# Time mixing in groups of two pairs of heads, issued by a timetable, with the keys projected ahead of it

## The chip, the cores and the metric

The kernel runs on one core of one Trainium2 chip. The metric is the device time of one execution in microseconds (us); the time of a kernel is the median of its runs. Five engines run side by side, each through its own list of instructions in that list's order: TensorE (PE in the profile: matrix products into PSUM; its weight loads are shown as PEld), VectorE (DVE), ScalarE (ACT), GpSimd (POOL) and SyncE (SP, which here only issues DMAs). They wait for each other by semaphores.

## The reference

The program is a trunk of two layers over one sequence of 256 tokens with a width of 2048. Layer 0 is RWKV-7 time mixing, layer 1 is chunked band attention over keys and values that are projected once; each is followed by a squared-ReLU MLP of width 8192. Every sub-layer has an RMS norm in front, shifted and scaled by vectors that come from a condition `c` through `c @ w_ada` (twelve such vectors of 2048 in the two layers, two more for the shared keys), and a gate from the same product on its output. All is f32. The change concerns time mixing:

```
xr, xw, xk, xv, xa, xg = [h + (shift(h) - h) * mu[j] for j in range(6)]
r, k, v = xr @ w_r, xk @ w_k, xv @ w_v
w_log = -softplus(-(w0 + tanh(xw @ w1) @ w2)) - 0.5
a = sigmoid(a0 + (xa @ a1) @ a2);  g = sigmoid(xg @ g1) @ g2
kk = normalized(k * k_k);  k = k * (1 + (a - 1) * k_a);  decay = exp(-exp(w_log))
for t in range(256):                      # 32 heads of 64, S is 64 x 64
    sa = S @ (-kk[t])
    S  = S * decay[t] + sa (kk[t] * a[t])' + v[t] k[t]'
    y[t] = S @ r[t]
y = groupnorm(y) * ln_w + ln_b + sum(r * k * r_k) * v
out = (y * g) @ w_o
```

## The kernel before

**Dense products.** A weight tile of 128x1024 f32 (half of the 2048 rows that one output tile of 128 needs, in eight blocks of 128x128) arrives by one DMA of 512 KB in a buffer `raw`. ScalarE rounds it to `wH`, VectorE makes the rest `wL = raw - wH` (`halves`, lines L360 and L363), and the activations are split in the same manner (`aHL`). For each block TensorE multiplies `wH` by both parts of the activation, 512 columns (L394), and `wL` by the upper part, 256 columns (L395). Such a pair of products is called a step here: an output tile of 128 takes 16 steps, a weight half 8. There are 6 buffers `raw` and 3 each of `wH` and `wL`.

**The condition's vectors.** `ada` takes one tile of 128x1024 of `w_ada` through a `raw` buffer, and VectorE adds it, scaled, to `acc` (L423). Sixteen tiles give half a vector; `ada_sum` then adds over the partitions with 32 small products. There are 384 tiles. Calls of `ada()` are strewn over the whole kernel, and `ada_need(...)` runs what is missing of a vector at once before its use.

**Time mixing.** Two heads fill the 128 partitions and are a pair; there are 16 pairs. The recurrence runs in 4 chunks of 64 tokens. `Pair` has three stages, written as generators: `early` (decays, normalized keys: long chains of elementwise work with `s` buffers), `invert` (the Gram products of keys, `gr`, and the inverse of a triangular matrix of 64 by doubling: five levels, each a product of 32x32 tiles, a copy `xs` on ScalarE, a second product, an addition to `u` and a transpose `tt` on VectorE), and `late` (the state `zs` from chunk to chunk, `chn`, the outputs `py`, the norm and the gate). In a period of 16 slots one pair is projected (`proj_steps`: `k` and `r`, 32 steps), the pair before it is in `early`, the one before that in `invert`, the one before that in `late`. There are 19 periods; in the last three, parts of the output projection (`out_steps`) take the place of the projections. `ADA_SLOTS` puts six tiles of `w_ada` in each period from the third.

**Order.** The code only says what depends on what. A scheduler that goes by the order of the code and by its own estimates sets the order of every engine's list; `issue_after` holds the small products and the dense steps of neighbouring slots together on TensorE.

The stage before time mixing projects `v` and ends at 221.7 us in the trace; after it come the output projection (`out_proj`), the first MLP, the attention and the second MLP.

Of the kernel before, what the change touches and what calls it, by code (L numbers as in the profile page):

```python
# [17 lines left out]
P = 128  # L18
D = 2048
T = 256  # L20
# [12 lines left out]
        "w0", "a0", "k_k", "k_a", "r_k", "ln_w", "ln_b"]  # L33
# [3 lines left out]
def _constants():  # L37
# [23 lines left out]
    p = np.arange(P)  # L61
    bones = (p[:, None] // C == p[None, :] // C).astype(np.float32)
    put("bones", bones)
# [10 lines left out]
class Pair:  # L74
# [3 lines left out]
    EARLY = 8  # L78

    def __init__(self, body, j, v, tw, ta, tg, e01):  # L80
        self.b, self.j, self.v, self.tw, self.ta, self.tg, self.e01 = body, j, v, tw, ta, tg, e01
        self.heads = (slice(0, C), slice(C, P))

    def s(self, name="s", bufs=10):
        return self.b.pw.tile([P, T], F32, tag=name, bufs=bufs, name=name)

    def big(self, name, bufs):
        return self.b.pw.tile([P, 4, P], F32, tag=name, bufs=bufs, name=name)

    @staticmethod  # L90
    def ch(t):
        return t.rearrange("p (c t) -> p c t", t=C)

    def each(self, o, lhsT, rhs):
        for c in range(4):
            for K in self.heads:
                self.b.nc.tensor.matmul(o(c)[K], lhsT(c)[K], rhs(c)[K], start=True, stop=True)  # L97

    def tiles(self, o, lhsT, rhs, pairs):

        for c in range(4):
            for R, K in pairs:
                self.b.nc.tensor.matmul(o[QS[K], c, :], lhsT[QS[R], c, :], rhs[QS[R], c, :], start=True, stop=True,  # L103
                                        tile_position=(H * R, H * K))

    def parts(self, func, src, scale=1.0):

        nc, pw = self.b.nc, self.b.pw
        H, L = (pw.tile([P, T], F32R, tag=n, bufs=2, name=n) for n in ("sH", "sL"))
        nc.scalar.activation(H, src, func, scale=scale)  # L110
        if func != AF.Copy:
            t = self.s("pt", 2)
            nc.scalar.activation(t, src, func, scale=scale)
            src = t
        nc.gpsimd.tensor_tensor(out=L, in0=src, in1=H, op=ALU.subtract)  # L115
        return H, L

    def head_sums(self, ps, parts):
        for i, t in enumerate(parts):
            self.b.nc.tensor.matmul(ps, self.b.bones, t, start=(i == 0), stop=(i == 1))  # L120

    def early(self):
        b, nc, j, k, r, v, s, ch = self.b, self.b.nc, self.j, self.k, self.r, self.v, self.s, self.ch
        pw, vec, cst, e01 = b.pw, b.vec, b.cst, self.e01
        lw = pw.tile([96, 2, P], F32, tag="lw", bufs=2, name="lw")
        nc.sync.dma_start(out=lw, in_=b.d["lora2"][j, :96, 0:2])
        self.lg = pw.tile([P, 2, P], F32, tag="lg", bufs=2, name="lg")
        nc.sync.dma_start(out=self.lg, in_=b.d["lora2"][j, :, 2:4])
        z = b.psm()
        nc.tensor.matmul(z[:, 0:T], lw[:, 0, :], self.tw, start=True, stop=True)  # L130
        nc.tensor.matmul(z[:, T:2 * T], lw[:, 1, :], self.ta, start=True, stop=True)

        sw, a = s(), s()
        for o, at, b0 in ((sw, 0, "w0"), (a, T, "a0")):
            nc.vector.tensor_scalar(out=o, in0=z[:, at:at + T], scalar1=vec(b0, j), scalar2=-80.0,
                                    op0=ALU.add, op1=ALU.max)
            nc.scalar.activation(o, o, AF.Exp, scale=-1.0)
        yield
        sq = self.parts(AF.Square, k, vec("k_k", j))
        for o in (sw, a):  # L140
            nc.scalar.activation(o, o, AF.Ln, bias=b.col(C_ONE))
        nc.scalar.activation(sw, sw, AF.Exp, scale=-1.0, bias=b.col(C_MHALF))
        nc.scalar.activation(a, a, AF.Exp, scale=-1.0)
        yield
        pss = b.psm()[:, :T]
        self.head_sums(pss, sq)
        cum = s()
        nc.vector.tensor_tensor_scan(out=cum, data0=cst("reset"), data1=sw, initial=0.0, op0=ALU.mult, op1=ALU.add)
        e0, e1 = e01[:, :, 0:C], e01[:, :, 1:C + 1]
        nc.scalar.activation(e1, ch(cum), AF.Exp, scale=-1.0)  # L150
        e2 = s()
        nc.scalar.activation(e2, cum, AF.Exp)
        self.pc = pw.tile([P, 4, 1], F32, tag="pc", bufs=3, name="pc")
        nc.gpsimd.tensor_copy(self.pc, e01[:, :, C:C + 1])
        yield
        rs, ss, rr = s(), s(), s()
        nc.vector.tensor_scalar(out=ss, in0=pss, scalar1=1e-24, scalar2=None, op0=ALU.max)
        nc.scalar.activation(rs, ss, AF.Ln)
        nc.scalar.activation(rs, rs, AF.Exp, scale=-0.5)
        nc.scalar.activation(rr, rs, AF.Square)  # L160
        km = s()
        nc.gpsimd.tensor_scalar(out=km, in0=a, scalar1=-1.0, scalar2=vec("k_a", j), op0=ALU.add, op1=ALU.mult)
        self.bh, self.kh = s("bh", 2), s("kh", 2)
# [927 lines left out]
```

## Time and profile before

| | us |
|---|---|
| median of 3 runs (2776.5 to 2784.27) | 2779.97 |
| the profiled execution | 2773.6 |
| its span | 2771.8 |
| projection of `v` and what lies before it | 0 to 221.7 |
| time mixing, up to the last pair's output | 221.7 to 761.6 |
| rest of the output projection | 761.6 to 839.7 |
| first MLP | 839.7 to 1593.2 |
| attention | 1593.2 to 2037.9 |
| second MLP and end | 2037.9 to 2771.8 |

The profiled execution stands 0.23% under the median. Stages were cut where the first instruction of the next begins (the first dense step, the last write of `v`, the first normed tile of the next norm). A trace shows each instruction with its start and duration, the idle time before it and what ended that. An f32 product is recorded twice, so that 16 products show as x32. Ends of products are modelled: two that follow each other overlap in the records, so the cost of one is the distance to the start of the next.

### The profile page before, as it was taken

What the parts mean: (1) busy time and instruction counts of PE and PEld (TensorE: products, weight loads), DVE (VectorE), ACT (ScalarE), POOL (GpSimd) and SP (SyncE); (2) the same over time, 40 slices, a digit from 0 to 9 for tenths busy, and PEclk for the clock granted to TensorE, in tenths of its full rate; (3) what the DMA queues carried; (4) which work ended last, traced back from release to release, by engine and by line L of the source; (5) the groups of instructions that cost most, each with busy time, mean ns of one, the idle gap of its engine ahead of it and who ended that gap; (6) DMA issues with size and microseconds to landing.
All of it is one profiled execution on the core that took longest, in us unless ns stands there. A gap on an engine that the chain in (4) does not pass through costs nothing.

```text
span 2771.8 us, 57644 instructions
## 1 busy us (share of the span) xinstructions
PE 2653.9 (96%) x23402; PEld 2217.6 (80%) x23402; DVE 2087.3 (75%) x3098; ACT 1260.9 (45%) x2214; POOL 301.8 (11%) x416
## 2 busy tenths in 40 slices
PE   6998999999998999999999899999989999999997
PEld 3677777777887888888888788877878888888886
DVE  4568778878889888888788896799786566665665
ACT  2345555556344434344344354465444344443444
POOL 0003443443220000000000200000100000000002
PEclk9999999999999999999999999999999999999999
DMA  9886556555687888888888868888876555555553
GB/s 297 269 281 193 169 171 196 176 176 162 216 302 243 298 308 305 300 314 296 299 306 302 304 218 282 268 293 268 279 242 216 187 186 186 187 183 189 185 188 122
DMA packets 217387, 662.60 MB, mean 239 GB/s; under 512 B 21408, under 2 KB 68896, under 8 KB 217120
## 3 DMA queue, kind: packets, MB, share of 16 engines
q1 hardware_dynamic: 215056, 656.36, 71.5%
q8 instruction: 184, 3.01, 0.4%
q10 hardware_dynamic: 2064, 2.54, 0.3%
q14 instruction: 83, 0.68, 0.1%
HBM read 656.72 MB, written 2.10 MB: 238 GB/s over the span
## 4 chain that ended last, share of the span: by engine, by line
PE 76%; DVE 9%; DMA 7%; issue 4%; POOL 1%; ACT 1%; DVEq 0%; SPq 0%; ACTq 0%; POOLq 0%
PE pj L394 40%; PE pj L395 20%; DMA raw<-w_ada 5%; DVE wL L363 3%; DVE acc L423 2%; PE iv L103 2%; PE gr L97 1%; DMA raw<-w_ada_kv 1%; PE m L625 1%; DVE un L504 1%; PE o L383 1%; PE ms L97 1%; POOL sL L115 1%; PE chn L276 1%; DVE aHL L506 1%
## 5 line engine op out<-in xcount | busy, mean ns | idle before, releaser
L394 PE MATMUL pj<-aHL,wH 128*128 128x512 f32 x3712 | 1353.5, 405 | 26.0 <-DVE aHL L506 22.4
L360 ACT CAST wH<-raw 128x1024 fp32r<-128x1024 f32 x772 | 807.0, 1047 | 949.4 <-PE pj L394 622.1
L363 DVE TENSOR_TENSOR wL<-raw,wH 128x1024 fp32r<-128x1024 f32 x772 | 946.1, 1228 | 290.7 <-ACT wH L360 288.8
L395 PE MATMUL pj<-aHL,wL 128*128 128x256 f32 x3712 | 1049.3, 283 | 7.5 <-DVE wL L363 7.2
L394 PEld LDWEIGHTS pj<-aHL,wH 128*128 128x128 f32 x3712 | 700.3, 189 | 199.2 <-issue 28.0
L394 PE MATMUL pj<-hHL,wH 128*128 128x512 f32 x2048 | 722.0, 397 | 4.5 <-DVE hHL L882 4.5
L395 PEld LDWEIGHTS pj<-aHL,wL 128*128 128x128 f32 x3712 | 705.3, 190 | 14.6 <-DVE wL L363 11.9
L395 PE MATMUL pj<-hHL,wL 128*128 128x256 f32 x2048 | 574.3, 281 | 4.6 <-DVE wL L363 4.5
L423 DVE SCALAR_TENSOR_TENSOR acc<-raw,ct,acc 128x1024 f32<-128x1024 f32 x360 | 470.4, 1307 | 139.8 <-DMA raw<-w_ada 104.0
L394 PEld LDWEIGHTS pj<-hHL,wH 128*128 128x128 f32 x2048 | 384.3, 188 | 97.9 <-DVE hHL L882 6.7
L395 PEld LDWEIGHTS pj<-hHL,wL 128*128 128x128 f32 x2048 | 386.8, 189 | 8.1 <-DVE wL L363 7.7
L482 POOL TENSOR_TENSOR ss<-ss,sq 128x256 f32<-128x256 f32 x56 | 65.0, 1160 | 1599.7 <-ACT sq L481 1599.4
L901 DVE SCALAR_TENSOR_TENSOR x<-pj,mod,x 128x256 f32<-128x256 f32 x256 | 123.1, 481 | 51.7 <-PE pj L395 48.8
L881 ACT CAST hHL<-t 128x256 fp32r<-128x256 f32 x128 | 51.4, 403 | 67.6 <-DVE t L880 67.3
L625 PE MATMUL m<-rawa,crep 128*32 128x256 f32 x512 | 47.4, 449 | 17.5 <-DMA rawa<-w_ada 16.9
L481 ACT ACTIVATE sq<-x 128x256 f32<-128x256 f32 x60 | 25.0, 418 | 70.5 <-DVE x L901 39.6
L880 DVE SCALAR_TENSOR_TENSOR t<-t 128x256 f32<-128x256 f32 x128 | 53.9, 422 | 3.0
L882 DVE TENSOR_TENSOR hHL<-t,hHL 128x256 fp32r<-128x256 f32 x128 | 53.4, 418 | 0.6 <-ACT hHL L881 0.5
L862 DVE TENSOR_TENSOR t<-pj,t 128x256 f32<-128x256 f32 x128 | 53.2, 417 | 0.0
L239 POOL TENSOR_TENSOR al<-da,csts 128x128 f32<-128x128 f32 x64 | 40.7, 647 | 67.4 <-PE iv L103 62.7
L861 ACT COPY t<-pj 128x256 f32<-128x256 f32 x128 | 46.6, 366 | 0.0
L685 PE MATMUL t<-aHL,wH 128*128 128x256 f32 x128 | 38.1, 298 | 5.8 <-DVE v L693 3.6
(230 smaller groups left out, 2483.0 us busy)
## 6 DMA issues: line engine op xcount, KB each, us to landing
raw<-w_ada SPq DMA_DIRECT2D x320, 512.0 KB, 4.7
raw<-w_up SPq DMA_DIRECT2D x256, 512.0 KB, 4.9
raw<-w_down SPq DMA_DIRECT2D x256, 512.0 KB, 4.3
rawa<-w_ada SPq DMA_DIRECT2D x64, 512.0 KB, 6.8
raw<-w_ada_kv SPq DMA_DIRECT2D x64, 512.0 KB, 5.4
raw<-w_k SPq DMA_DIRECT2D x32, 512.0 KB, 4.2
raw<-w_r SPq DMA_DIRECT2D x32, 512.0 KB, 4.7
raw<-w_o SPq DMA_DIRECT2D x32, 512.0 KB, 5.2
```

The costliest lines, as they stand in the source:

```text
L97: self.b.nc.tensor.matmul(o(c)[K], lhsT(c)[K], rhs(c)[K], start=True, stop=True)
L103: self.b.nc.tensor.matmul(o[QS[K], c, :], lhsT[QS[R], c, :], rhs[QS[R], c, :], start=True, stop=True, tile_position=(H * R, H * K))
L360: nc.scalar.copy(Hf, raw)
L363: eng.tensor_tensor(out=Lf, in0=raw, in1=Hf, op=ALU.subtract)
L394: nc.tensor.matmul(ps, H[:, i, :], a(kt), start=(kt == 0), stop=False)
L395: ins = nc.tensor.matmul(ps[:, 0, :], L[:, i, :], a(kt)[:, 0, :], start=False, stop=(kt == KT - 1))
L423: nc.vector.scalar_tensor_tensor(out=acc, in0=raw, scalar=ck, in1=acc, op0=ALU.mult, op1=ALU.add)
L482: (eng or nc.gpsimd).tensor_tensor(out=self.ss, in0=self.ss, in1=sq, op=ALU.add)
L625: nc.tensor.matmul(ps[g:g + 32, part, :W], crep[:, kt, :], raw[:, i, :], start=(part == 1 and kt < 4), stop=(part == 0 and kt >= KT - 4), ...
L880: nc.vector.scalar_tensor_tensor(out=t, in0=t, scalar=0.0, in1=t, op0=ALU.max, op1=ALU.mult)
L882: nc.vector.tensor_tensor(out=h[:, 1, :], in0=t, in1=h[:, 0, :], op=ALU.subtract)
L901: nc.vector.scalar_tensor_tensor(out=x, in0=ps[:, i, :], scalar=self.mods[(layer, 5)][:, n:n + 1], in1=x, op0=ALU.mult, op1=ALU.add)
```

## The change

Time mixing is written anew. A `Quad` holds two pairs, so that elementwise work goes over 512 columns where it went over 256, and each batch of small products has twice as many. There are 8 quads. A quad's work is a table of steps, each with a slot from -8 to 45 and a rank within the slot (`at(slot, rank)`); a quad starts 20 slots after the one before, so that slots 20 to 39 of one lie beside slots 0 to 19 of the next, and slots 40 to 45 beside slots 0 to 5 of the one after that. TensorE's list has exactly the order of the code (`InOrder`, `STRICT`); the other engines' lists are the scheduler's as before.

All 16 key tiles are projected ahead of the first quad (256 steps, with 23 tiles of `w_ada` among them), then `r` of quad 0; the timetable's `UNITS` hold 32 steps per quad for `r` of the next. Sums over heads are f32 products with ones in place of two rounded ones with `bones`, so that `parts` is gone. The Gram products are four of 64 columns for two of 128. Copies of `da` move from ScalarE to GpSimd. `raw` has 4 buffers in place of 6 up to the end of time mixing, and 8, 8, 6 and 8 in the stages behind it (`more_raw`). In time mixing 77 tiles of `w_ada` are taken (23 with the keys, 54 in the slots), where it was 102; the vectors needed later are completed by `ada_need`, with 3 tiles before the first MLP, 11 in it, and 11 before the attention's output projection.

```diff
+class InOrder:
+    def __getattr__(self, name):
+        f = getattr(self.to, name)
+        return (lambda *args, **kw: self.tc.keep_in_program_order(f(*args, **kw))) if callable(f) else f
...
+class Quad:
+    PERIOD = 20
+    LAST = 45
...
+    def each(self, o, lhsT, rhs):
+        for c in range(8):
+            for K in self.heads:
+                self.b.mm(o[K, c, :], lhsT(c)[K], rhs(c)[K], start=True, stop=True)
...
+    def head_sums(self, t):
+        ps = self.b.psm()
+        for K in self.heads:
+            self.b.mm(ps[K], self.b.cst("ones")[K, 0:C], t[K], start=True, stop=True)
+        return ps
...
+        @at(7, 1)
+        def _():
+            dve.scalar_tensor_tensor(out=self.rr, in0=self.rr, scalar=-0.5, in1=self.ss, op0=ALU.mult, op1=ALU.mult)
+            for j, o in self.pairs(self.a):
+                pool.tensor_scalar(out=o, in0=o, scalar1=-1.0, scalar2=vec("k_a", j), op0=ALU.add, op1=ALU.mult)
...
+        @at(12, 1)
+        def _():
+            self.A = self.s("A", 1)
+            act.copy(ch(self.A), self.gram(self.bh, 0))
+            self.da = self.half("da")
+            for i, K in enumerate(self.quarters):
+                n = H * (i % 2)
+                pool.tensor_copy(self.da[K], ch(self.A)[K, :, n:n + H])
+            dve.tensor_tensor(out=self.ar, in0=self.gram(self.bh, 1), in1=ui[:, :, C:P], op=ALU.mult)
...
+        for l in range(1, 6):
+            at(14 + 2 * l, 2)(first(l))
+            at(15 + 2 * l, 2)(second(l))
...
+        for c in range(4):
+            for i, f in enumerate(chunk(c)):
+                at(first + 3 * c + i, 0)(f)
...
 class Body:
-    RAW_BUFS = 6
     W_BUFS = 3
-    DRAIN_STEPS = (14, 14, 16)
-    ADA_SLOTS = (1, 3, 6, 9, 11, 14)
+    UNITS = (0, 0, 0, 0, 5, 5, 0, 4, 3, 4, 3, 0, 0, 0, 0, 5, 3, 0, 0, 0)
+    HALVES, LAST_HALVES = (6, 7, 13, 16), (7, 10, 13, 16)
+    ADA_SLOTS = (0, 2, 12, 15, 18, 19)
+    STRICT = ("tensor",)
...
+    def raw_tile(self):
+        self.nraw += 1
+        if self.more and self.nraw % (self.more[1] + 4) >= 4:
+            return self.more[0].tile([P, HK * P], F32, tag="raw", bufs=self.more[1], name="raw")
+        return self.wp.tile([P, HK * P], F32, tag="raw", bufs=4, name="raw")
...
+            half(), half()
+            for n, _ in enumerate(dense(range(KT), xk, lambda i: k[:, i, :])):
+                if n % HK == 0:
+                    half()
+                if n % 11 == 10:
+                    self.ada()
...
+            for slot in range(-8, end - Quad.PERIOD + Quad.LAST + 1):
+                while steps and steps[0][0] == slot:
+                    steps.pop(0)[3]()
...
+                for _ in range(self.UNITS[at] if p < NQ_ else 2 * (at > 5)):
+                    next(big, None)
```

What the change does to the lists is shown at three places. The first is a level of the inverse on TensorE in the middle of time mixing; before, `iv<-tt,al` and `iv<-u,xs` are the first and the second product of a level of one pair, and chunk products and dense steps (`pj`) stand between them.

```order
L103 MATMUL iv<-tt,al 32x32 x16
L293 MATMUL chn<-bk 64x64
L295 MATMUL chn<-sa,bk 64x64 x2
L304 MATMUL py<-ar,sa 64x64 x2
L394 MATMUL pj<-aHL,wH 128x512
L395 MATMUL pj<-aHL,wL 128x256
L103 MATMUL iv<-u,xs 32x32 x16
```

After, the same place from the first product of level 2 to that of level 5 (`sl,csts` and `s,csts` are sums over heads, `tw`, `ta` and `tg` the low-rank products):

```order
L79 MATMUL iv<-tt,al 32x32 x32
L79 MATMUL ms<-sl,csts 64x512 x2
L79 MATMUL iv<-u,xs 32x32 x32
L79 MATMUL iv<-tt,al 32x32 x32
L79 MATMUL ms<-tw,lw 128x256 x2
L79 MATMUL iv<-u,xs 32x32 x32
L79 MATMUL ms<-ta,lw 128x256 x2
L79 MATMUL ms<-s,csts 64x512 x2
L79 MATMUL iv<-tt,al 32x32 x32
L79 MATMUL iv<-u,xs 32x32 x32
L79 MATMUL ms<-tg,lg 128x256 x4
L79 MATMUL iv<-tt,A 32x32 x16
```

No dense step is left between the products of levels 2 to 4, and two products of the inverse stand next to each other in two places. The second place is VectorE's list beside it: `u<-u,iv` is the addition of a level, `tt<-u` its transpose. Before:

```order
L252 TENSOR_TENSOR u<-u,iv 128x128
L235 STREAM_TRANSPOSE tt<-u 128x128
L363 TENSOR_TENSOR wL<-raw,wH 128x1024
L157 TENSOR_SCALAR s<-ms 128x256
L300 SCALAR_TENSOR_TENSOR zs<-zs,pc,chn 128x64
L170 SCALAR_TENSOR_TENSOR s<-s,k 128x256
```

After, from the end of the Gram work to level 2 (`hold<-ms,csts` 128x512 is `ar` and 128x8x64 is half of `mk`, both read Gram products; `sl<-py,vecs,sl` is a step of the norm of the quad before):

```order
L334 TENSOR_TENSOR hold<-ms,csts 128x512
L345 TENSOR_TENSOR u<-u,csts 128x256
L313 STREAM_TRANSPOSE tt<-u 128x256
L615 SCALAR_TENSOR_TENSOR acc<-raw,ct,acc 128x1024
L441 SCALAR_TENSOR_TENSOR zs<-zs,pc,chn 128x64 x2
```

```order
L383 TENSOR_TENSOR hold<-ms,csts 128x8x64
L368 TENSOR_TENSOR u<-u,iv 128x256
L383 TENSOR_TENSOR hold<-ms,csts 128x8x64
L313 STREAM_TRANSPOSE tt<-u 128x256
L615 SCALAR_TENSOR_TENSOR acc<-raw,ct,acc 128x1024
L368 TENSOR_TENSOR u<-u,iv 128x256
L474 SCALAR_TENSOR_TENSOR sl<-py,vecs,sl 128x256
L313 STREAM_TRANSPOSE tt<-u 128x256
```

The transposes of levels 1 and 2 now stand behind an operation that reads other products, and the state `zs` of the third chunk stands behind the first steps of the next quad's inverse. The third place is SP's list in the first MLP, where the upward half ends. Before:

```order
L350 DMA raw<-w_up 128x1024 x2
L350 DMA raw<-w_ada_kv 128x1024
L350 DMA raw<-w_down 128x1024 x2
L350 DMA raw<-w_ada_kv 128x1024
L350 DMA raw<-w_down 128x1024 x2
```

After:

```order
L542 DMA raw<-w_up 128x1024 x2
L542 DMA raw<-w_ada 128x1024 x11
L542 DMA raw<-w_ada_kv 128x1024
L542 DMA raw<-w_down 128x1024 x2
L542 DMA raw<-w_ada_kv 128x1024
```

Eleven tiles that were spread over time mixing now lie in one piece ahead of the first weights of `w_down`.

More of the change, by code (lines that the diff above doesn't have):

```diff
@@ new lines, in all_halves, with half @@
+            def all_halves():
+                for n in ("w_k", "w_r"):
+                    for j in range(NPAIR):
+                        for i in range(KT // HK):
+                            yield lambda: self.halves(self.raw(d[n][j][:, i * HK * P:(i + 1) * HK * P]))
+                for n, lo, hi in first + second:
+                    yield lambda: self.weight_part(d["w_o"][n], lo, hi)[0]
+            halves, self.ready = all_halves(), []
+            def half():
+                f = next(halves, None)
+                if f:
+                    self.ready.append(f())
```

692 lines of the change are left out of this document (390 added, 302 removed).

## The prediction

> **What bounds the kernel now.** I read the page first, then the busy times by stage, then TensorE's instructions in time, then the groups by form.
>
> ```profile
> span 2771.8 us, 57644 instructions
> PE 2653.9 (96%) x23402; PEld 2217.6 (80%) x23402; DVE 2087.3 (75%) x3098; ACT 1260.9 (45%) x2214; POOL 301.8 (11%) x416
> ```
>
> By stage (columns: window, then busy us and count for PE, PEld, DVE, ACT, POOL, the granted clock, the DMA share, GB/s):
>
> ```profile
> 221.70:371.20 149.50, 139.34 (x2306) 110.25 (x2307) 121.52 (x221) 82.09 (x216) 62.89 (x77) 0.98 0.59 189
> 371.20:677.60 306.40, 302.11 (x5811) 233.60 (x5811) 245.41 (x461) 166.84 (x466) 125.83 (x167) 0.99 0.55 173
> 677.60:761.60 84.00, 82.49 (x1470) 69.67 (x1470) 70.56 (x119) 36.17 (x100) 20.06 (x31) 1.00 0.65 209
> 761.60:839.70 78.10, 64.95 (x435) 56.73 (x434) 62.98 (x71) 31.34 (x42) 17.44 (x14) 0.91 0.88 300
> 839.70:1593.20 753.50, 731.92 (x4802) 634.33 (x4802) 635.64 (x796) 322.78 (x418) 18.02 (x20) 0.99 0.87 298
> ```
>
> Time mixing (the first three rows, 539.9 us) is bound by TensorE: in the steady part it is idle for 306.4 - 302.1 = 4.3 us. The DMAs have room there (0.55) and little in the two rows behind it (0.87). What TensorE spends its time on is seen in its list. The first two rows mark the same point of two periods ten pairs apart; the others give distances from start to start.
>
> ```profile
> 371.17 0.44 PE L103 MATMUL iv<-tt,co 32*32 32x32 f32 x16
> 677.61 0.44 PE L103 MATMUL iv<-tt,co 32*32 32x32 f32 x16 [0.16 <-DVE tt L235]
> ...
> 222.04 0.28 PE L395 MATMUL pj<-aHL,wL 128*128 128x256 f32 x1
> 222.39 0.28 PE L395 MATMUL pj<-aHL,wL 128*128 128x256 f32 x1
> ...
> 251.14 0.68 PE L97 MATMUL ms<-csts,s 64*64 64x64 f32 x16 [0.43 <-POOL s L208]
> 251.75 0.50 PE L394 MATMUL pj<-aHL,wH 128*128 128x512 f32 x1
> ...
> 280.38 1.10 PE L97 MATMUL ms<-csts,s 64*64 64x64 f32 x32
> 281.41 0.50 PE L394 MATMUL pj<-aHL,wH 128*128 128x512 f32 x1
> ...
> 503.50 0.45 PE L103 MATMUL iv<-tt,al 32*32 32x32 f32 x32
> 503.89 0.50 PE L394 MATMUL pj<-aHL,wH 128*128 128x512 f32 x1
> 504.22 0.28 PE L395 MATMUL pj<-aHL,wL 128*128 128x256 f32 x1
> 504.34 0.40 PE L394 MATMUL pj<-aHL,wH 128*128 128x512 f32 x1
> 504.58 0.28 PE L395 MATMUL pj<-aHL,wL 128*128 128x256 f32 x1
> 504.78 0.33 PE L276 MATMUL chn<-bk,mk 64*64 64x64 f32 x4
> ```
>
> - A pair takes 306.44 / 10 = 30.6 us, two pairs 61.3.
> - A dense step takes 0.35 us. The 32 steps of a pair are 11.2 us, so 19.4 us of its 30.6 go to small products, of which 0.4 is idle.
> - A batch of 64x64 products costs 0.61 us when it holds 8 and 1.03 when it holds 16: the second half costs 0.42.
> - Going from dense to small and back costs 0.18 us: the product after a small batch takes 0.33 to the next in place of 0.24, the one before a batch 0.20 in place of 0.12.
>
> **The change, part by part.**
>
> *TensorE's own work.* Small products of a quad, priced by these rows: levels, eight batches of 0.39 x 1.69 and two of 0.37 x 1.69 (1.69 is 1.03 / 0.61), 6.5 us; three transposes of 1.03, 3.1; Gram products, four of 1.03, 4.1; the chunks, 28 groups of 0.17 + 0.105 (504.78 to the next group is 0.17, a fourth of 0.42 for each group's second half), 7.7; three sums over heads of two products of 512 columns side by side, eight times 64 columns of 0.105 plus 0.1, 2.9; eight low-rank products of 256 columns, 0.42 each, 3.4; sums of `ada` 0.2. That is 27.9. With 32 dense steps (11.2) and 8 blocks of them in the list (1.4) a quad has 40.5 us of TensorE, and the keys in front take 11.2 us per quad more: 51.7 in place of 61.3. Over 8 quads this saves 77 us. The saving is real work, since TensorE hardly idles before.
>
> *The new waits.* TensorE can no longer take what is ready: its list is fixed, and the other engines' lists decide how long it stands. Durations that count:
>
> ```profile
> L363 DVE TENSOR_TENSOR wL<-raw,wH 128x1024 fp32r<-128x1024 f32 x768 | 944.2, 1232 | 288.9 <-ACT wH L360 287.1
> L423 DVE SCALAR_TENSOR_TENSOR acc<-raw,ct,acc 128x1024 f32<-128x1024 f32 x360 | 470.4, 1307 | 139.8 <-DMA raw<-w_ada 104.0 <-DMA raw<-w_ada_kv 34.7
> L261 DVE TENSOR_TENSOR mk<-gr,csts 128x512 f32<-128x512 f32 x16 | 11.0, 686 | 1.9 <-PE gr L97 1.0
> L213 DVE TENSOR_TENSOR ar<-gr,csts 128x256 f32<-128x256 f32 x16 | 6.7, 420 | 6.0 <-PE gr L97 5.9
> L235 DVE STREAM_TRANSPOSE tt<-u 128x128 f32<-128x128 f32 x80 | 24.2, 303 | 0.7
> L229 ACT COPY bk<-ms 128x512 f32<-128x512 f32 x16 | 9.3, 581 | 2.6 <-PE ms L97 2.5
> L314 ACT ACTIVATE sl<-sl 128x256 f32<-128x256 f32 x16 | 6.6, 412 | 0.2
> L247 POOL COPY uf<-u 32x128 f32<-32x128 f32 x64 | 33.1, 517 | 2.5
> L222 POOL TENSOR_TENSOR u<-da,csts 128x128 f32<-128x128 f32 x16 | 12.2, 761 | 84.9 <-ACT da L219 84.9
> L162 POOL TENSOR_SCALAR s<-s,vecs 128x256 f32<-128x256 f32 x16 | 14.9, 931 | 0.0
> ```
>
> At the new sizes I estimate 0.42 us for an addition `u` (a 128x256), 0.44 for its transpose, 0.65 for an exponential of 512, 0.6 for a copy of `da` and 1.1 for `u` on GpSimd, and 0.1 for each hop. Six waits of a quad follow from the lists:
>
> 1. First product of level 2: its transpose stands behind the second half of `mk`. The Gram product ends 1.03 us after level 1, `mk` takes 0.69, the transpose 0.44, hops 0.2: 2.4 us after level 1, of which 1.03 is covered. Wait 1.3.
> 2. First product of level 3: its transpose stands behind `sl`, and `sl` behind a logarithm and an exponential (1.3) after the sum over heads. 0.1 + 1.3 + 0.48 + 0.44 + 0.2 after that sum, 0.6 covered: 1.9.
> 3. Second product of level 4: its copy `xs` stands in ScalarE's list behind five functions of the next quad (3.3 us), which start when the low-rank product has passed VectorE: 1.5 to 2.3.
> 4. First use of the inverse: `uf` stands on VectorE behind an operation that waits for two of GpSimd's 0.93: 1.0.
> 5. Chunk 1: the state `zs` stands behind some 5 us of the next quad's early work, 1.3 more where a tile of `w_ada` lies in it: 0.9 to 2.2.
> 6. Chunk 3: `zs` stands behind the Gram chain (copy 0.6, four `da` 2.4, `u` 1.1, addition and transpose 0.9, in some quads `acc` 1.3) while TensorE has some 4.2 us to do: 1.6 to 2.9.
>
> Sum 8.2 to 11.6; I take 9 (the tile of `w_ada` lies in the chain of about every other quad) for seven quads, since the first and the last have half each: +63. The bounds are 2 us a quad (only the two places where products of the inverse stand next to each other, 16 us) and 12 (96 us). Who waits behind TensorE there is everything: the dense steps stand in the same list.
>
> *The clock.* A stall costs more than itself, as four windows of time mixing show:
>
> ```profile
> 261.80:265.21 3.41, 0.99 (x73) 0.82 (x77) 3.41 (x9) 1.48 (x5) 0.53 (x1) 1.00 0.72 251
> 265.21:268.62 3.41, 3.41 (x70) 2.65 (x70) 3.29 (x6) 0.98 (x3) 2.82 (x3) 0.50 0.53 159
> 302.80:306.21 3.41, 2.04 (x21) 1.77 (x21) 1.36 (x4) 1.39 (x4) 3.02 (x6) 1.00 0.85 290
> 306.21:309.62 3.41, 3.41 (x48) 2.53 (x47) 2.18 (x6) 0.52 (x2) 0.12 (x1) 1.00 0.19 74
> ```
>
> A window of 3.41 us in which TensorE was busy for 0.99 is followed by one at half clock; after 2.04 busy the clock stays. So waits of about 2 us that fall into one window cost up to 1.7 us more. I estimate two such windows a quad, half of it lost in waits that follow: +14, between 0 and 8 x 3 x 1.7 = 41. The Trainium skill (TensorE: Matmul & The Clock Gate, the table on what matters for kernels) only asks for no idle gaps over about 3 us; by that rule no wait above would lower the clock, this term would be 0 and the time 14 us lower. The row at 261.80, where no single gap reaches 3 us, says otherwise.
>
> *The keys in front.* 256 steps take 89.6 us; meanwhile 32 weight tiles and 23 of `w_ada` pass through 4 buffers.
>
> ```profile
> raw<-w_ada SPq DMA_DIRECT2D x320, 512.0 KB, 4.7
> raw<-w_k SPq DMA_DIRECT2D x32, 512.0 KB, 4.2
> ```
>
> A buffer is held for 4.2 to 4.7 us of landing and 1.3 to 2.5 of use, about 6.8 with the issue; 55 tiles through 4 buffers take 55 x 6.8 / 4 = 94 us. I take +8 with the hops, between 0 and 25 (a buffer held for 8.3).
>
> *Moved tiles of `w_ada`.* In time mixing DMAs and VectorE lose 25 tiles and nobody waits for them. The two bursts of 11 stand in SP's list ahead of weights: at 300 GB/s 11 x 1.75 = 19 us, while TensorE has three prepared halves (8.4 us) and some tail. I estimate 5 us each: +10, between 0 and 22. The eight buffers of the first MLP could give back at most its idle 753.5 - 731.9 = 21.6 us, most of it at the norms; 0, down to -6. The last stages, the first 221.7 us (SP's list is the same) and 16 steps that move from time mixing to the output projection cost 0.
>
> Sum: -77 + 63 + 14 + 8 + 10 = +18. On the profiled execution's 2773.6 that is 2792; it stands 6 us under the median of the runs, so in medians 2798. I say 2795.
>
> **The rivals.** *The waits are short, and it is faster.* If VectorE has run ahead where I let it start from behind, half of the waits go and with them the low-clock windows: -77 + 31 + 3 + 6 + 8 = -29, 2750. For it speaks that VectorE has less to do per pair: its 245.4 us for ten pairs hold 12 tiles of `w_ada` per two pairs, now 6. Against it: five of the six waits stand behind an operation that itself waits for TensorE, ScalarE or GpSimd, and lie in each quad's list. It decides at 7.4 us of waits and lost clock per quad (77 - 18 = 59 over 8).
>
> *The clock falls at every long wait.* Three windows a quad, fully on the path: +41 in place of 14, 2822. For it: waits 2, 3, 5 and 6 are each about 2 us. Against: a wait that straddles two windows is halved.
>
> *No change.* Waits of 5.5 a quad with one window: -77 + 44 + 7 + 8 + 10 = -8 to +8 with the bursts' bounds, 2780.
>
> **How the numbers follow.** My forecast 0.38, the lower clock 0.12, no change 0.14, faster 0.36. A difference under 0.3% (8 us) cannot be told from none. The case of the forecast alone has 2789 to 2815. The range reaches from the faster case with waits of 2 to 3 us (2735) to the lower clock with slow keys (2845). Faster 0.36, same 0.14, slower 0.50.
>
> **What would show it.** By stage: keys from 222 to about 320 with a DMA share near 0.9; quads of 49 to 53 us from one `iv<-tt,A` to the next, of which TensorE idles about 9; in its waits `tt`, `xs`, `zs` and `uf` as releasers, with 1 to 3 us each; the granted clock of time mixing under 0.98; an idle TensorE where `w_down` begins and where the attention's output projection begins. Quads of 44 us would make the faster rival right; quads of 40 us would mean that TensorE never waits and the time falls under my range.

## The result, and the profile after

The changed kernel is slower: 2879.99 us (median of 4 runs, 2874.2 to 2888.56) against 2778.23 (2774.77 to 2784.27). The ratio is 1.0366, with an interval of 1.0334 to 1.0399. The forecast was 2795 in a range up to 2845: the sign was right, the size was not. The profiled execution took 2888.6 us, the longest of the four.

The head of its page:

```profile
span 2886.8 us, 57668 instructions
PE 2660.6 (92%) x23882; PEld 2227.8 (77%) x23882; DVE 2066.3 (72%) x2893; ACT 1196.3 (41%) x1845; POOL 199.2 (7%) x296
```

All engines but TensorE are less busy than before, TensorE is as busy as before, and the span is 115 us longer. Busy times by stage (columns as in the prediction): keys, begin of the first quad, seven quads, the last quad's end, rest of the output projection, first MLP, attention.

```profile
221.70:329.30 107.60, 96.12 (x577) 81.62 (x577) 71.64 (x85) 40.11 (x60) 0.99 (x2) 0.97 0.77 255
329.30:402.00 72.70, 52.69 (x894) 41.09 (x893) 48.66 (x62) 28.50 (x48) 11.64 (x17) 0.78 0.52 169
402.00:782.10 380.10, 316.41 (x8024) 253.27 (x8024) 242.16 (x389) 140.16 (x279) 92.55 (x136) 0.91 0.35 110
782.10:812.60 30.50, 29.58 (x421) 25.95 (x421) 13.44 (x24) 9.91 (x22) 0.00 (x0) 0.98 0.34 108
812.60:897.60 85.00, 73.57 (x524) 63.63 (x523) 70.29 (x81) 33.78 (x45) 16.29 (x14) 0.89 0.87 307
897.60:1673.80 776.20, 742.41 (x4802) 639.05 (x4802) 654.99 (x811) 321.37 (x418) 19.95 (x20) 0.98 0.87 299
1673.80:2139.80 466.00, 433.83 (x2818) 358.41 (x2818) 372.52 (x585) 219.94 (x418) 22.61 (x72) 0.95 0.79 261
```

The attention of the kernel before, between the same marks (first tile of the one norm to first tile of the next):

```profile
1593.20:2024.40 431.20, 417.38 (x2754) 349.38 (x2754) 358.95 (x574) 219.47 (x418) 22.45 (x72) 0.99 0.81 267
```

| stage | before | after | more |
|---|---|---|---|
| time mixing | 539.9 | 590.9 | 51.0 |
| rest of the output projection | 78.1 | 85.0 | 6.9 |
| first MLP | 753.5 | 776.2 | 22.7 |
| attention | 431.2 | 466.0 | 34.8 |
| all else | 969.1 | 968.7 | -0.4 |

A quad takes 380.1 / 7 = 54.3 us from one `iv<-tt,A` to the next. TensorE is idle for (380.1 - 316.4) / 7 = 9.1 us of it. The granted clock is 0.91: 18% of the 380.1 us ran at half clock, which lost 34 us of work, 4.9 per quad. What is left is 54.3 - 9.1 - 4.9 = 40.3 us of work. What time mixing takes beyond eight quads is 48.9 us after (72.7 + 380.1 + 30.5 - 8 x 54.3) and 49.7 before (539.9 - 16 x 30.64), so the quads and the keys hold the whole difference. Whom TensorE waited for in these seven quads (us in total, times, longest):

```profile
PE iv L79 <- DVE tt L313: 25.1, 17, 2.7
PE chn L79 <- DVE zs L441: 17.8, 8, 5.0
PE chn L79 <- DVE zs L438: 8.1, 6, 2.1
PE iv L79 <- issue: 5.7, 3, 3.5
PE iv L79 <- ACT xs L353: 5.5, 7, 1.8
PE iv L79 <- DVE mod L631: 1.7, 1, 1.7
PE chn L79 <- DVE uf L373: 0.3, 2, 0.2
```

The longest of these waits shows what stands in VectorE's list (timeline of VectorE, then the product of TensorE that waited):

```profile
586.83 1.49 DVE L615 SCALAR_TENSOR_TENSOR acc<-raw,ct,acc 128x1024 f32<-128x1024 f32 x1 [0.37 <-DMA raw<-w_ada]
588.24 0.68 DVE L334 TENSOR_TENSOR hold<-ms,csts 128x512 f32<-128x512 f32 x1
590.20 0.85 DVE L345 TENSOR_TENSOR u<-u,csts 128x256 f32<-128x256 f32 x1 [1.28 <-POOL u L339]
591.08 0.45 DVE L313 STREAM_TRANSPOSE tt<-u 128x256 f32<-128x256 f32 x1
593.42 1.28 DVE L615 SCALAR_TENSOR_TENSOR acc<-raw,ct,acc 128x1024 f32<-128x1024 f32 x1 [1.89 <-DMA raw<-w_ada]
594.62 0.47 DVE L441 SCALAR_TENSOR_TENSOR zs<-zs,pc,chn 128x64 f32<-128x64 f32 x2
...
595.23 0.38 PE L79 MATMUL chn<-hold 64*64 64x64 f32 x4 [5.00 <-DVE zs L441]
```

VectorE stood 1.89 us at a tile of `w_ada` that had not landed. Behind the tile stood `zs`, behind `zs` TensorE, and in TensorE's fixed list the dense steps, which needed neither. The next window of 3.4 us ran at half clock:

```profile
588.60:592.00 3.40, 1.63 (x32) 0.75 (x26) 1.61 (x3) 0.59 (x1) 2.80 (x5) 1.00 0.82 278
592.00:595.40 3.40, 0.17 (x5) 0.20 (x7) 1.98 (x4) 0.00 (x0) 0.00 (x0) 1.00 0.08 33
595.40:598.80 3.40, 3.40 (x24) 2.90 (x22) 0.64 (x2) 0.27 (x1) 0.00 (x0) 0.50 0.52 159
```

### The profile page after: what moved, and what is told of

The parts are those of the page before. It is cut to its first block, busy times and chain, and to the rows that moved or that the text cites. A ratio compares the mean times of both kernels' runs of the same rounds, so it can differ in the third digit from the quotient of the medians.

```text
span 2886.8 us, 57668 instructions
## 1 busy us (share of the span) xinstructions
PE 2660.6 (92%) x23882; PEld 2227.8 (77%) x23882; DVE 2066.3 (72%) x2893; ACT 1196.3 (41%) x1845; POOL 199.2 (7%) x296
## 5 line engine op out<-in xcount | busy, mean ns | idle before, releaser
L587 PE MATMUL pj<-aHL,wL 128*128 128x256 f32 x3488 | 989.8, 284 | 14.8 <-DVE wL L555 14.7
L586 PEld LDWEIGHTS pj<-aHL,wH 128*128 128x128 f32 x3488 | 662.4, 190 | 204.2 <-issue 24.7
L587 PEld LDWEIGHTS pj<-aHL,wL 128*128 128x128 f32 x3488 | 667.1, 191 | 24.1 <-DVE wL L555 23.4
L79 PE MATMUL pj<-aHL,wL 128*128 128x256 f32 x256 | 74.9, 293 | 0.6 <-DVE wL L555 0.6
L79 PEld LDWEIGHTS pj<-aHL,wH 128*128 128x128 f32 x256 | 51.4, 201 | 15.7 <-DVE wL L555 1.6
L820 PE MATMUL m<-rawa,crep 128*32 128x256 f32 x512 | 47.5, 450 | 16.3 <-DMA rawa<-w_ada 15.8
L79 PEld LDWEIGHTS iv<-tt,al 32*32 32x32 f32 x2048 | 23.8, 115 | 43.6 <-issue 42.9
L79 PE MATMUL iv<-tt,al 32*32 32x32 f32 x2048 | 27.3, 204 | 31.0 <-DVE tt L313 28.4
```

Of the source, the lines that this page charges most:

```text
L79: return (lambda *args, **kw: self.tc.keep_in_program_order(f(*args, **kw))) if callable(f) else f
L586: nc.tensor.matmul(ps, H[:, i, :], a(kt), start=(kt == 0), stop=False)
L587: ins = nc.tensor.matmul(ps[:, 0, :], L[:, i, :], a(kt)[:, 0, :], start=False, stop=(kt == KT - 1))
L820: nc.tensor.matmul(ps[g:g + 32, part, :W], crep[:, kt, :], raw[:, i, :], start=(part == 1 and kt < 4), stop=(part == 0 and kt >= KT - 4), ...
```

## The experiments

Stage times are those of their profiled executions, whole times are medians, and each ratio is to the kernel before on the same chip.

### The tiles of `w_ada`

**The changed kernel with the tiles back in time mixing.**

```diff
-    ADA_SLOTS = (0, 2, 12, 15, 18, 19)
+    ADA_SLOTS = (0, 2, 5, 8, 12, 15, 16, 18, 19)
```

> The changed kernel with nine tiles of w_ada per walk of the slots in place of six, so that time mixing takes 104 tiles (102 before the change, 77 after it). Theory A: the first MLP and the attention move 300 and 260 GB/s and have no room, so each tile that left time mixing costs there its transfer, 0.524 MB at 300 GB/s, 1.75 us, or more. Then the rest of the output projection, the first MLP and the attention together fall from 1328 us to 1263 to 1280, time mixing stays at 590 to 605, and the time is 2820 to 2840. Rival: these stages are longer because of something else (the other numbers of raw buffers, the half clock): they stay above 1310 and the time is 2865 or more.

2894.56 us, ratio 1.0413 (1.0381 to 1.0445): theory A fell, and the rival came out, since the three stages behind time mixing still took 1315 us together. Time mixing took 615.5 us, 25 more for 25 tiles more. The attention fell by 25 to 441.1, the output projection's rest was 90.4, and the first MLP did not fall at all:

```profile
924.00:1707.80 783.80, 746.42 (x4802) 640.21 (x4802) 640.70 (x797) 321.05 (x418) 17.29 (x20) 0.98 0.84 287
```

What the attention had lost lay at its end. The first row holds the last softmaxes and the first steps behind them in the changed kernel, the second the same 50 us with the tiles back:

```profile
1990.00:2040.00 50.00, 40.12 (x274) 28.82 (x273) 43.98 (x86) 20.90 (x60) 1.48 (x12) 0.79 0.79 254
```

```profile
2012.00:2062.00 50.00, 48.77 (x363) 37.89 (x364) 45.85 (x94) 28.62 (x74) 3.02 (x13) 1.00 0.78 255
```

In the changed kernel VectorE has the forced tiles in its list between the steps of the last softmaxes; TensorE idles for 10 us there and the clock falls to 0.79. With the tiles back it idles for 1.2 us and keeps its clock.

**The kernel before with 24 tiles fewer in time mixing.**

```diff
-                    if slot in self.ADA_SLOTS and p >= 2:
+                    if slot in self.ADA_SLOTS[::2 if p % 2 else 1] and p >= 2:
```

> The kernel before, with every second period of time mixing taking three tiles of w_ada in place of six, so that 24 tiles move out of time mixing and nothing else changes. Theory A (no room behind time mixing): time mixing stays within 5 us of 540, the stages from the rest of the output projection to the end of the attention grow from 1263 us by 40 to 65, and the time is 2818 to 2845. Rival (the tiles are absorbed, what the changed kernel loses there comes from its buffers): growth under 20, 2780 to 2800.

2788.94 us, ratio 1.0039 (1.0023 to 1.0055). The rows are time mixing, the rest of the output projection, and the first MLP:

```profile
217.40:745.70 528.30, 518.37 (x9512) 409.33 (x9512) 403.24 (x771) 284.28 (x779) 188.09 (x274) 0.99 0.51 164
745.70:848.50 102.80, 68.73 (x506) 60.32 (x506) 87.07 (x93) 32.22 (x45) 18.22 (x14) 0.81 0.88 308
848.50:1598.30 749.80, 733.82 (x4738) 634.66 (x4738) 639.15 (x796) 322.95 (x418) 16.62 (x14) 0.99 0.87 301
```

Time mixing became 11.6 us shorter, which theory A had not said; the output projection 24.7 and the attention 11.3 longer. A tile costs 0.5 us in the old time mixing, 24.7 / 18 = 1.4 in the output projection, and the first MLP was not touched. The whole, 11 us more, came where the rival had it; the three stages behind time mixing grew by 32 us, between the two.

**No tile in the quads.** `ADA_SLOTS = ()`.

> The changed kernel with no tile of w_ada in the slots of the quads (23 remain among the keys); the other 54 follow in the stages behind. It is run for the length of time mixing. Theory F: a good part of the waits of TensorE is VectorE standing at a tile of w_ada that has not landed, with zs or tt behind it; 27 tiles more had made time mixing 25 us longer, so 54 fewer make it 35 to 55 us shorter: 536 to 556 us in place of 591, with quads of 47 to 49.5 us. Rival (the waits come from the order of the quads' own steps): 575 or more, quads of 52.5 or more. The stages behind take 54 tiles more, so the whole time is 2890 to 2940 by either.

2919.05 us, ratio 1.0514 (1.0481 to 1.0548). Time mixing took 543.6 us, as theory F has it. Seven quads, their waits, and the output projection that then has to take 65 tiles:

```profile
387.60:729.40 341.80, 295.07 (x7832) 239.19 (x7832) 190.85 (x343) 139.42 (x279) 85.92 (x136) 0.97 0.18 58
...
762.70:928.80 166.10, 75.90 (x716) 66.60 (x714) 127.06 (x131) 34.50 (x47) 16.46 (x14) 0.71 0.87 304
```

```profile
PE iv L79 <- DVE tt L313: 25.9, 16, 2.5
...
PE chn L79 <- DVE zs L441: 6.3, 7, 0.9
```

A quad takes 48.8 us: 6.7 of idle time and 1.5 of lost clock (0.03 of 48.8), in place of 9.1 and 4.9; 40.6 of work are left, close to the 40.3 with the tiles. The wait for `tt` is the same as with the tiles, so it belongs to the lists; that for the later `zs` falls from 17.8 to 6.3 and never exceeds 0.9. VectorE took 31 tiles in the stage in place of 78 (some of the forced ones still fall into it): 47 tiles cost 47.3 us, 1.0 each. Of the 5.8 us by which a quad loses less, 3.4 are the clock; how much of these the tiles caused is looked at below.

**No tile among the keys.**

```diff
-                if n % 11 == 10:
-                    self.ada()
```

> The changed kernel without the 23 tiles of w_ada among the keys; they follow behind. It is run for the length of the keys, 107.6 us from the first product of a key to the first of r, of which the 256 steps are 89.6. Theory I: the 55 tiles that pass through four buffers bound this stage; with 32 it takes 90 to 95 us. Rival: half or more of the 18 us are the start (the first weights of the keys land late) and the half clock behind it: 99 or more. The whole is 2880 to 2920 by either, since 23 tiles come later.

2915.43 us, ratio 1.0498 (1.0472 to 1.0525). The keys alone:

```profile
221.30:311.70 90.40, 89.61 (x505) 77.29 (x506) 48.45 (x64) 41.41 (x63) 0.99 (x2) 1.00 0.58 189
```

TensorE is idle for 0.8 us and the first step of `r` begins after 91.8, in place of 107.6: theory I. The 23 tiles between 32 weight tiles cost 15.8 of the 18.0 us that the keys took beyond their 89.6 us of work, 0.7 each. That they cost it at the four buffers and not at the DMAs was not tried by itself. Time mixing as a whole did not become shorter, 597.3 in place of 590.9 us: with the same tiles in their slots the quads took 56.6 us, and the cause of that stays open.

### TensorE's list and its clock

**The dense steps spread over the waits.**

```diff
-    UNITS = (0, 0, 0, 0, 5, 5, 0, 4, 3, 4, 3, 0, 0, 0, 0, 5, 3, 0, 0, 0)
-    HALVES, LAST_HALVES = (6, 7, 13, 16), (7, 10, 13, 16)
+    UNITS = (0, 2, 0, 0, 4, 2, 0, 0, 5, 0, 0, 2, 0, 0, 8, 0, 0, 4, 0, 5)
+    HALVES, LAST_HALVES = (5, 10, 14, 18), (7, 10, 13, 16)
```

> The changed kernel with the same 32 dense steps per quad at other slots: 4 and 5 before the first products of levels 2 and 3, 2 and 4 inside levels 3 and 4, 5 and 8 before the chunk products that read the state, 2 each elsewhere. Theory B: TensorE stands 9.1 us per quad idle because its fixed list has no dense step where it waits, and the half clock that follows costs 4.9 more. Then the idle time falls to 3 to 5 us per quad, the granted clock of the quads rises from 0.91 to 0.96 or more, quads take 45 to 49 us in place of 54.3, and the time is 2800 to 2840. Rival: the releasers are late by their own lists and by whatever is put ahead of them, so the waits only move: quads of 52 or more, 2865 to 2890.

2863.51 us, ratio 1.0304 (1.0267 to 1.0341), quads of 52.8: between the two, nearer to the rival.

```profile
395.70:765.10 369.40, 308.04 (x8020) 249.83 (x8020) 241.19 (x388) 141.00 (x280) 92.98 (x136) 0.93 0.35 111
```

The waits of levels 2 and 3 and of the chunks were filled, but three new ones of 7.5 to 9.0 us appeared ahead of `iv<-tt,A`. At one of them (VectorE's timeline, and the DMAs in the same time):

```profile
491.00 1.26 DVE L232 TENSOR_TENSOR_SCAN s<-csts,s 128x256 f32<-128x256 f32 x2
500.80 1.28 DVE L615 SCALAR_TENSOR_TENSOR acc<-raw,ct,acc 128x1024 f32<-128x1024 f32 x1 [8.54 <-DMA raw<-w_ada]
```

```profile
497.00:500.00 3.00, 0.00 (x0) 0.00 (x0) 0.00 (x0) 0.00 (x0) 0.00 (x0) 0.84 0.06 25
```

For three microseconds no engine did anything, and the DMA engines were busy for 0.06, which is what one of sixteen would be.

**The low-rank weights in 128 rows.** Just ahead of that tile stood the load `lw`: 97 rows, 96 of the low-rank weights and one for the bias, that the change appended.

```diff
-            self.lw = pw.tile([97, 2, 2, P], F32, tag="lw", bufs=1, name="lw")
-            b.nc.sync.dma_start(out=self.lw, in_=b.d["lora2"][self.q, :97, 0:2])
+            self.lw = pw.tile([P, 2, 2, P], F32, tag="lw", bufs=1, name="lw")
+            b.nc.sync.dma_start(out=self.lw, in_=b.d["lora2"][self.q, :, 0:2])
```

> The changed kernel, with the low-rank weights lw of a quad loaded as 128 rows (the rows behind 97 are zero and aren't used) in place of 97. In the run with the spread steps the 194 packets of 2 KB of this load went one after the other at 84 ns each for 8.5 us, while everything else on the DMAs was done, and a tile of w_ada issued behind it landed after 11 us; VectorE stood at that tile with a transpose of the inverse behind it. Theory D: a load of 97 rows is not spread over the DMA engines, one of 128 is. Then the 256 packets take about 1 us, VectorE's waits for tiles of w_ada in the quads (26 us) fall by a third or more, quads take 51 to 53.5 us in place of 54.3 and the time is 2855 to 2876. Rival: the load is slow by its small packets and not by its rows: packets as before one after the other, 2876 to 2890.

2865.6 us, ratio 1.0320 (1.0298 to 1.0342): theory D in the packets and in the whole time, though the quads fell only from 54.3 to 53.5. The load has 97 packets of 2 KB (the expectation counted them twice). In the changed kernel those of the load issued at 396.4 us start between 0.9 and 9.5 us after the issue, here the 128 of the load issued at 389.6 between 1.0 and 2.2. The issue groups of the changed kernel and of this one; the latter's has a landing time:

```profile
lw<-lora SPq DMA_DIRECT2D x8, 194.0 KB
```

```profile
lw<-lora SPq DMA_DIRECT2D x8, 256.0 KB, 2.9
```

The Trainium skill says this (DMA: Bandwidth & Descriptors, the section on why a DMA increments its semaphore by 16 and not by 1): a DMA runs on the largest number of engines, up to 16, that divides the slowest dimension of both sides, so 97 rows give one engine. The packets agree. The prediction had counted this load at nothing.

**Products without use in the waits.**

```diff
+        for slot, rank, n in ((18, 1.5, 3), (20, 1.5, 3), (25, 1.5, 1), (29, -1, 2), (35, -1, 4)):
+            at(slot, rank)(fill(n))
```

> The changed kernel with 13 products without use per quad (256 columns of f32, about 0.42 us each, 5.5 us in all, into the unused half of the buffer iv) just ahead of the five places where TensorE waits: 3 before level 2, 3 before level 3, 1 before the second product of level 5, 2 before chunk 1 and 4 before chunk 3. Theory C: half of what the waits cost is the half clock behind them, 4.9 us per quad; with TensorE busy in the waits the granted clock of the quads goes from 0.91 to 0.97 or more and quads take 49 to 52 us: 2840 to 2865, although TensorE has more to do. Rival: the clock costs nothing on the path, since TensorE waits for other engines anyway; quads stay at 54 or grow by what the products stick out: 2875 to 2905.

2887.35 us, ratio 1.0391 (1.0354 to 1.0428), quads of 54.2.

```profile
400.20:779.70 379.50, 344.34 (x8208) 274.20 (x8208) 241.74 (x389) 140.06 (x278) 96.38 (x136) 0.97 0.34 110
```

By the time the rival was right, by its reason not. The clock rose to 0.97, so that a quad lost 1.6 us to it in place of 4.9, and the idle time fell from 9.1 to 5.0. Of these 7.4 us the products took 5.6 (13 of 0.43) and five switches, at the 0.18 of the prediction, 0.9; 0.9 stay unexplained. With TensorE busy in the waits the clock rose, but the work that was only there for that cost as much as it saved.

**TensorE's list by the scheduler.** `STRICT = ()`.

> The changed kernel with TensorE's list set by the scheduler, as those of the other engines are and as it was before the change (STRICT empty). Theory G: TensorE's fixed list is what exposes the waits; a list by the scheduler has dense steps in them, TensorE idles under 4 us per quad, quads take 46 to 50 us and the time is 2810 to 2850. Rival: the waits follow from the lists of VectorE and ScalarE and from tiles that land late, which the scheduler's estimates don't know either: quads of 52 or more, 2865 or more.

2847.9 us, ratio 1.0263 (1.0237 to 1.0289), 32 us less than the changed kernel; quads of 51.0.

```profile
396.10:753.00 356.90, 319.76 (x8001) 252.29 (x8001) 239.86 (x383) 139.54 (x279) 92.49 (x129) 0.94 0.36 115
```

That is between theory G and its rival. A quad has 5.3 us idle and 3.1 of lost clock (0.06 of 51.0); the work rises from 40.3 to 42.6. More switches between dense and small products are a part of the rise: TensorE's list has 12 blocks of dense steps per quad here and 8 in the changed kernel, which at 0.18 is 0.7 of the 2.3 us. The rest stays open. The fixed list costs more than it saves, but the scheduler's list meets the same tiles.

**Both edits.**

> The changed kernel with both edits that shortened it: TensorE's list by the scheduler (32 us less than the changed kernel alone) and the low-rank weights loaded in 128 rows (14 us less). If the two are separate mechanisms they add up to 46 us: time mixing 545 to 549 us and 2828 to 2842 in all, still some 55 us over the kernel before, since the stages behind time mixing keep what they lost (768 to 776 in the first MLP, 460 to 467 in the attention). Rival: the scheduler's list already hides the late loads, then the second edit gives nothing more: 2845 to 2855.

2842.29 us, ratio 1.0229 (1.0205 to 1.0252): 5.6 us less than with the scheduler's list alone, between the two expectations. The two intervals overlap, so that the second edit gives anything on top is not shown. Time mixing was 550.3 in place of 558.2; the first MLP (771.7) and the attention (469.8) kept their loss.

### The first MLP

**Six buffers in place of eight**, at three places:

```diff
-                s2.enter_context(self.more_raw(4))
+                s2.enter_context(self.more_raw(2))
```

> The changed kernel with six raw buffers in the rest of the output projection and in both MLPs, as before the change, in place of eight (the attention has six in both). With the tiles of w_ada back in time mixing the first MLP still took 784 us against 754 before the change, with as many tiles. Theory E: the eight buffers cost there 15 to 30 us (more weights in front of the tiles of w_ada in the queue, VectorE's list stands at them); with six the first MLP takes 750 to 762 us in place of 776 and the time is 2855 to 2868. Rival: the buffers are harmless, and the loss is the 14 tiles more and the burst ahead of w_down: the first MLP stays at 770 to 785, the time at 2872 to 2890.

2918.57 us, ratio 1.0510 (1.0474 to 1.0546). Theory E has the wrong sign: the first MLP took 813 us.

**The kernel before with its six buffers divided.**

```diff
+        tag, bufs = ("rawb", 2) if self.nraw % 6 >= 4 else ("raw", 4)
-        t = self.wp.tile([P, HK * P], F32, tag="raw", bufs=self.RAW_BUFS, name="raw")
+        t = self.wp.tile([P, HK * P], F32, tag=tag, bufs=bufs, name="raw")
```

> The kernel before, with its six raw buffers in two groups, four and two, that the tiles take in turn by their number (four in the one, then two in the other), as the changed kernel divides its buffers behind time mixing. With six buffers the changed kernel's first MLP took 813 us, with eight 776, with eight and as many tiles as before the change 784; the kernel before takes 754 with six in one group. Theory H: the division costs, because a tile waits for a buffer of its group while one of the other is free: the first MLP of this kernel takes 770 to 800 us and the whole 2800 to 2860. Rival: the division costs nothing, since the buffers come free in the order of the tiles anyway: first MLP 748 to 760, 2770 to 2790.

2792.23 us, ratio 1.0062 (1.0044 to 1.0080); first MLP 771, 18 more, as theory H has it, in a whole that grew by less: to divide six buffers costs something. The attention grew too, by 14 us from 431.2:

```profile
1598.60:2043.90 445.30, 423.65 (x2754) 351.73 (x2754) 358.65 (x573) 219.57 (x418) 22.15 (x72) 0.98 0.77 259
```

In the changed kernel the six buffers of the attention are divided in the same way, which may be the 10 us that it still takes more when the tiles are back (441.1); that was not tried by itself.

**The changed kernel with the tiles back and six buffers in one group.**

```diff
-        if self.more and self.nraw % (self.more[1] + 4) >= 4:
+        if self.more and (self.more[1] > 2 or self.nraw % (self.more[1] + 4) >= 4):
...
-                s2.enter_context(self.more_raw(4))
+                s2.enter_context(self.more_raw(6))
```

> The changed kernel with nine tiles of w_ada per walk (as in the run with the tiles back) and with six raw buffers in one group, apart from the four of time mixing, in the output projection of time mixing and in both MLPs. Its first MLP then differs from that of the kernel before in nothing but what the stages ahead leave behind. Theory H: it takes 748 to 762 us, in place of 784 with eight buffers in two groups, and the whole 2850 to 2872 in place of 2895. Rival (the loss comes from the order of the queue, which the scheduler made otherwise): 775 or more and 2885 or more.

2894.29 us, ratio 1.0411 (1.0376 to 1.0446); first MLP 787: the division is not what the changed kernel lost. The rows of the three, in this order:

```profile
902.30:1715.40 813.10, 753.87 (x4802) 643.55 (x4802) 654.22 (x810) 320.00 (x418) 15.87 (x20) 0.97 0.84 286
```

```profile
827.20:1598.60 771.40, 741.92 (x4802) 637.15 (x4802) 637.16 (x797) 321.43 (x418) 19.40 (x20) 0.99 0.85 291
```

```profile
920.20:1707.50 787.30, 747.18 (x4802) 639.83 (x4802) 641.51 (x800) 321.80 (x418) 15.95 (x20) 0.98 0.84 285
```

The last has as many buffers in one group as the kernel before, three tiles of `w_ada` more (172 for 169), and in this stage the same order of weights and tiles in SP's list; it still takes 34 us more, spread over the whole stage. What differs is VectorE's list, where tiles of `w_ada` stand between other steps of the hidden tiles. That this is the cause was not tried, so most of the 22.7 us of the first MLP stays open. The burst of eleven tiles is at most a part: in the changed kernel TensorE stands for 6.3 us where `w_down` begins, and about 8 us are lost by then, but with the tiles back, without the burst, some 7 are lost by the same point.

## Why the prediction was wrong

By its own terms, with the measured ones taken for eight quads:

| term | predicted | bounds | measured | how |
|---|---|---|---|---|
| TensorE's work | -77 | | -78 | a quad 40.3 in place of 40.5 |
| waits | +63 | 16 to 96 | +73 | 9.1 x 8 (64 for the seven quads that were forecast) |
| clock | +14 | 0 to 41 | +39 | 4.9 x 8 |
| keys | +8 | 0 to 25 | +18 | 107.6 - 89.6 |
| behind time mixing | +10 | 0 to 22 | +64 | 6.9 + 22.7 + 34.8 |
| sum | +18 | | +116 | the two profiles differ by 115 |

The sum is off by 98 us: 54 of them lie behind time mixing, 25 in the clock, 10 each in the waits and the keys.

**The work was right.** What a quad takes beside idle time and lost clock is 40.3 us in the changed kernel and 40.6 without tiles, where 40.5 were forecast. The parts of that sum were not measured one by one.

**The waits were right in size, with some luck, and mostly in place.** The per-quad sum was 9 and is 9.1. Level 2 was put at 1.3 and took 1.6, level 3 at 1.9 and took 1.7, chunk 1 at 0.9 to 2.2 and took 1.4, chunk 3 at 1.6 to 2.9 and took 2.2, each over six quads. The copy `xs` makes the fifth level wait, for about 1, and not the fourth, where 1.5 to 2.3 were forecast; `uf` costs nothing in place of 1.0. That the sum still agrees is luck: what these two were too high is made up by the others and by 0.8 us of gaps for which the profile shows no releaser (`issue`). The faster rival fell with this: the waits are not short, because they stand behind operations that themselves wait.

**The clock was mis-sized.** The step "two such windows a quad, half of it lost in waits that follow" gave 14; the rival with three windows fully on the path gave 41, and 39 is what was lost. In the seven quads the clock stood at half for 66 us, in twelve stretches; that is 2.8 windows of 3.4 us a quad. Only three of the stretches, a window each, follow the sixth wait. Its mean was right, but it is 0.9 us without a tile of `w_ada` that is late and about 4 to 5 with one, and the long ones empty a whole window: the prediction let the tile lie in the chain of every other quad at VectorE's 1.3 us and never let VectorE wait for its landing. Two more windows follow chunk 1, and the other seven stretches, 49 of the 66 us, follow waits at the levels of the inverse, most of them 1.7 to 2.1 us long. The rule of the Trainium skill that was weighed there (TensorE: Matmul & The Clock Gate, the table on what matters for kernels) fits the long sixth waits; it is not enough for a window with 1.67 of 3.4 us busy around one gap of 1.7 us, which half clock followed too:

```profile
547.60:551.00 3.40, 1.67 (x98) 1.50 (x86) 2.41 (x6) 1.56 (x4) 0.00 (x0) 1.00 0.00 0
551.00:554.40 3.40, 3.40 (x70) 2.12 (x69) 1.56 (x3) 2.41 (x5) 0.00 (x0) 0.50 0.02 5
```

Without tiles the same wait of 1.7 us before level 3 is still there in four quads, but in three of them it lies across the border of two windows, and the clock stays. This is the first of the three, where TensorE is busy for 2.4 and 2.5 us of the two windows:

```profile
423.60:427.00 3.40, 2.43 (x132) 1.50 (x132) 0.50 (x3) 1.69 (x3) 0.64 (x1) 1.00 0.17 64
427.00:430.40 3.40, 2.49 (x133) 2.05 (x133) 2.56 (x6) 1.18 (x3) 0.00 (x0) 1.00 0.02 5
```

So the 3.4 us of clock per quad that the run without tiles gained are only in part the late tiles; how the quads fall on the windows is another part. The prediction names it ("a wait that straddles two windows is halved") but does not price it, and it can come out otherwise by chance.

**The step that failed is the one on the moved tiles**: "In time mixing DMAs and VectorE lose 25 tiles and nobody waits for them", and 5 us for each burst. Both halves were wrong. In time mixing TensorE does pay for the tiles, 0.7 to 1.0 us each in the changed kernel and 0.5 in the old one: they are a price of the stage, and not filler. Whether the tiles land late there because time mixing has four buffers `raw` where it had six was not tried. Behind it a tile costs about its transfer, 1.4 to 1.8 us in the output projection, where 512 KB at 300 GB/s take 1.75, and eleven cost 25 us in the attention: there the burst was costed at the weights behind it in SP's list, but it lies in VectorE's list between the softmaxes. The stages of before had warned of it, with a DMA share of 0.88 in the rest of the output projection and 0.87 in the first MLP; the prediction quoted both and then priced only the two bursts.

The moved tiles are not all of the 64 us. With 25 tiles back in time mixing, the three stages behind it still take some 52 us more than in the kernel before. The prediction put everything but the bursts at nothing there, with 0 down to -6 for the eight buffers; of the 22.7 us of the first MLP most is open, and so are 10 of the 34.8 of the attention.

**The keys** were costed at the buffers, and their tiles of `w_ada` are 15.8 us of the excess of 18, where 8 were forecast. That the tiles lengthen the stage was right; that it is by the buffers fits, but was not shown by itself.

## What to carry to other kernels

An order fixed by hand on one engine is only as good as the lists of the engines that feed it. Price each wait with the landing of every transfer in those lists, not with the duration of the operation alone, and look at where it falls in the windows of the clock. Work that is strewn as filler has a price in each stage (here 0.5 to 2.3 us a tile); moving it is a trade between two such prices, and both must be read from the profile.

## What the runs showed of the hardware

A load of 97 rows of 2 KB went as 97 packets one after the other, 84 ns each, for some 8 us, with a DMA share of 0.06, one engine of sixteen. A tile of 512 KB issued right behind it landed after 10 to 11 us, where such tiles took 4.7 in the median of the kernel before. The 128 packets of a load of 128 rows started within 1.3 us.

In the changed kernel the stretches at half clock begin and end on one grid of 3.41 us. A wait of 1.7 us within one window of the grid was followed by half clock, and the same wait across a border was not.

The first MLP, with 169 to 172 tiles and the same products, took 750, 754, 771, 784 and 787 us in five kernels that differ in buffers and in the order of lists alone.
